# A hybrid attention / S5 / FFN block: more weight and staging buffers in the FFN, a rotated tile order, two products slice by slice

## The chip, the cores and the metric

One Trainium2 chip, one core. The kernel is timed as device microseconds of that core. Its engines are named as in the trace: PE (TensorE matmul) and PEld (its weight loads), DVE (VectorE), ACT (ScalarE), POOL (GpSimd), SP (SyncE, which only issues DMAs here).

## The reference

One encoder block on x of 1024 tokens by 1024 features, all in float32:

```python
h = rms(x, g_pre_mix) * (1 + sc1) + sh1
q_lat, kv_lat, k_rope_raw, u, gates = split(h @ w_in)
branch_a = mla(q_lat, kv_lat, k_rope_raw, ...)      # q = rms(q_lat) @ w_uq, 8 heads: 64 nope + 32 rope
branch_b = s5(u, ...)                                # two scans, then gelu, w_glu
mixed = (sigmoid(gates_a) * branch_a + sigmoid(gates_b) * branch_b) @ w_mix_out
x = x + gt1 * rms(mixed, g_post_mix)
h = rms(x, g_pre_ffn) * (1 + sc2) + sh2
g, up = split(h @ w_ffn_in)                          # 2 x 2816 features, 22 slices of 128
f = (silu(g) * up) @ w_ffn_out
x = x + gt2 * rms(f, g_post_ffn)
```

sc, sh and gt are six vectors of length 1024 computed from a conditioning vector c.

## The kernel before

Everything is held transposed, features on the 128 partitions and tokens along the free axis, in two halves of 512 tokens. A float32 product is three fp32r matmuls (`mm3`, L203 to L205): weight's high part by data's high part, high by the data's low part (L204), and the weight's low part by data's high part (L205). So each weight tile and each operand is split first: the high part by ACT (a copy, `whi`, `fhi`, `mh`), the low part by DVE (a subtraction, `wlo`, `flo`). Each engine runs its instructions in the order in which the code records them, and an instruction that waits holds all that stand behind it.

Weights ahead of the late FFN come through `win`, a stream of the class `WStream` over the list `wl`: `win.get()` hands out the next weight, and on the way splits a further one (L185 on ACT, L67 on DVE) and loads later ones on SP. The list and the order of the `get` calls must agree.

Attention. `uq_nope` and `uq_rope` make the query tiles (four without rotation, two rotated), `kv_norm`, `k_rope` and `y_chain` are generators whose steps are interleaved with them. Then come the k and v products (`uk`, L1106, and `uv`). Behind the heads, the attention-out product takes eight output tiles in two halves, (m, h), and the mix product reads them all.

FFN. The 22 pairs (one slice of gate and one of up) stand in nine groups (`FGROUPS` 4, 2, 2, 2, 2, 2, 2, 2, 4). Group 0 goes plainly through `ffn_in(p, h)`: gate, then up, 24 matmuls each. Its first pair follows directly on `chain`, which makes the eight slices of the normed input (L1575 on ACT, L75 on DVE); between products, `tick()` runs one step of a backlog of such chains and `drain()` runs all that is left. Groups 1 to 8 go through `pair7`: both halves of a pair from seven block products over a split weight and data of half the depth (28 slices of three matmuls), with weight blocks A11, S2, S1, S3, A12, A22 and S4. Sums of weight blocks are POOL's (L1733 to L1744). The class `Blocks` keeps the list of these weight blocks and of the output weights behind each group (`O`, and `L` for the last), splits them (L1717 on ACT, L67 on DVE) some steps ahead, and loads them with DMAs from POOL's queue (L1703) into two raw tiles `wraw`. A raw tile is loaded again once its last block is split.

A pair ends in `ft` tiles (high and low part of the activated product, low half first, then high half; L1619). Behind each group, `out_tiles` multiplies all eight output tiles by the group's two pairs; ACT copies each of the 16 results into one of four staging tiles `fio` (L1661), and a POOL DMA adds it to `fd` in HBM (L1663). The last group's results are read together with `fd`, and finished by `final`: sums of squares (L1875 on ACT, L247 on PE), a norm, and per tile a product (DVE), the addition of x (POOL, L1918) and a store; loads and stores there are issued from ACT's queue (L149). The last group's columns are done in three parts: tokens of half 0, a first 256 of half 1, and the last 256. `drain()` stands between these parts, so that the five remaining steps of half 0's final are recorded ahead of the next part's work.

Of the kernel before, what the change touches and what calls it, by code (L numbers as in the profile page):

```python
# [17 lines left out]
P = 128  # L18
# [73 lines left out]
def _body(tc, a, out):  # L92
# [204 lines left out]
    wl += [(a["wuq"][i], 6 * P) for i in range(3)] + [(a["wuk"], 8 * P), (a["wuv"], 2 * HF)]  # L297
# [774 lines left out]
    def uq_rope():  # L1072

        w = win.get(2)
# [67 lines left out]
    for i in range(4):  # L1142
        if i % 2 == 0:
            w = win.get()
        uq_nope(i, w)
        next(kv_norm, None)
        if i == 2:
            next(krope)
        if i == 2:
            next(ych)  # L1150
    uqr = uq_rope()
    next(uqr)
    for _ in kv_norm:
        pass
    next(ych)
    for _ in uqr:
        next(ych)
# [225 lines left out]
    with ExitStack() as m_es:  # L1383
# [45 lines left out]
        for m in range(KD):  # L1429
            if m >= 4 and m % 2 == 0:  # L1430
                w = [win.get()]
            if m in (2, 4):
                win.split()
            for h in range(2):
                if m < 4:
                    ps = pss[m, h]
                    ao_mm(ps, w[m // 2], m, h, (3,))
                else:
                    ps = ps_b()
                    ao_mm(ps, w[0], m, h, range(4))  # L1440
                ao_out(ps, m, h)
            gm_load(m + 2)
            flush()
# [38 lines left out]
    def prod(ps, w, hi, lo, n, off=0):  # L1482
        for k in range(n):
            mm3(ps, w, hi(k), lo(k), off + k, k == 0, k == n - 1)
            if k % 2:
                tick()

# [134 lines left out]
    def ffn_in(p, h):  # L1622
# [9 lines left out]
        for w, ps in ((wg, pg), (wu, pu)):  # L1632
            prod(ps, w, lambda k: hi[:, k, :], lambda k: lo[:, k, :], KD)
# [7 lines left out]

    def f_tile():
        return half_tile(fp, "fio", 4)
# [38 lines left out]
    class Blocks:  # L1682


        def __init__(self, seq):
            self.seq, self.n, self.got, self.raw, self.hl = seq, 0, 0, [], []
            self.loads = []
            for kind, i, j in seq:
                if kind == "A11":
                    self.loads += [a["wfi"][2 * i], a["wfi"][2 * i + 1]]  # L1690
                elif kind == "O" and j % 2 == 0:
                    o = 2 * starts[i] * P
                    self.loads.append(a["wfo"][j:j + 2, :, o:o + HF].rearrange("m p c -> p m c"))
                elif kind == "L":
                    o = 2 * starts[i] * P
                    self.loads.append(a["wfo"][j, :, o:o + D])

        def load(self, n=1):
            for _ in range(n):
                if self.loads:  # L1700
                    t = wp.tile([P, D], F32, name="wraw", tag="wraw", bufs=2)
                    src = self.loads.pop(0)
                    G.dma_start(t.rearrange("p (m c) -> p m c", m=2) if len(src.shape) == 3 else t, src)  # L1703
                    self.raw.append(t)
# [18 lines left out]
        def advance(self, n):  # L1723

            while self.n < min(n, len(self.seq)):
# [3 lines left out]
                if kind == "A11":  # L1729
                    g, u = self.g, self.u = self.raw.pop(0), self.raw.pop(0)  # L1730
# [16 lines left out]
                elif kind == "S4":  # L1747
                    self.split(self.g[:, hi])
                    self.load(2)
                elif kind == "O":  # L1750
                    self.split(self.raw[0][:, halves[j % 2]])
                    if j % 2:
                        self.raw.pop(0)
                        self.load()
                else:
                    self.split(self.raw.pop(0), self.out() if j == 3 else None)
                    self.load()
# [77 lines left out]

    def pair7(p, prep):
# [21 lines left out]
        A_.activation(gl, gl, AF.Silu)  # L1858
        tt(p1, prod7(tops["T4"]), u3, ALU.add)
        tt(gl, gl, p1, ALU.mult)  # L1860
        ft_put(p, lo, gl)
        tt(u2, prod7(b22), u2, ALU.add)
# [65 lines left out]
    for kind, i, hs in units:  # L1928
# [9 lines left out]
        for m in range(0, KD, 2):  # L1938
            out_tiles(0, win.get(), [(m, h), (m + 1, h)], out_store, m == 0)
            if h and m == 4:  # L1940
                bl.load(2)
# [6 lines left out]
    for g in range(1, last + 1):  # L1948
        big_first = g % 2 == 0
        for n, p in enumerate(range(starts[g], starts[g + 1])):  # L1950
            if (n < 2) == big_first:
                if n % 2 == 0:
                    ft_big(1, p)
            else:
                ft_new(p)
            pair7(p, drain if p == starts[1] else tick)
# [4 lines left out]

    tt(gg2, ada[:, 40:48], g_post2, ALU.mult)
# [7 lines left out]
    for h, c0, n in ((0, 0, HF), (1, 0, QF), (1, QF, QF)):  # L1970
# [25 lines left out]
        drain()  # L1996
# [101 lines left out]
```

## Time and profile before

| | us |
|---|---|
| median of 3 runs | 1700.69 (1699.6 to 1703.08) |
| profiled execution | 1698.5 |
| its span in the trace | 1696.7 |
| PE busy | 1594.6, 94% of the span |
| DVE, ACT, POOL busy | 1084.4, 652.0, 408.9 |
| mean granted clock of TensorE | 0.978 |

The span runs from the first to the last instruction in the trace. A busy PE isn't PE at its peak: matmuls overlap, and each is listed with a modelled end. In a wait row, the time is what the engine stood idle ahead of the instruction; in a timeline row it stands in brackets, with the engine and line that ended it. The granted clock is a fraction of full speed, 1.00 for 2.4 GHz and 0.50 for 1.2 GHz.

### The profile page before, as it was taken

How to read it: one execution, taken by the hardware profiler on the slowest of the kernel's cores; microseconds unless marked ns; L12 is line 12 of the kernel's file. 1: busy time of each engine (PE TensorE's matmuls, PEld its weight loads, DVE VectorE, ACT ScalarE, POOL GpSimd, SP SyncE). 2: the span in 40 equal slices, each digit the busy share in tenths (PEclk: the TensorE clock that was granted, in tenths of full speed). 3: DMA queues.
4: the chain of work that ended last, by engine and by line, in shares of the span. 5: the costliest groups of instructions: out<-in, count | busy, mean ns of one | idle time of the engine just before them, and what ended most of it. 6: DMA issues, size and time to landing. Idle time of an engine off the chain costs nothing.

```text
span 1696.7 us, 20064 instructions
## 1 busy us (share of the span) xinstructions
PE 1594.6 (94%) x7318; PEld 1276.0 (75%) x7318; DVE 1084.4 (64%) x1785; ACT 652.0 (38%) x961; POOL 408.9 (24%) x470
## 2 busy tenths in 40 slices
PE   6989999999899999989999999999999999999994
PEld 6878888888688677757777777777777877777783
DVE  6978998977857778855646676625336335244655
ACT  4142313233621666663334444343333343333330
POOL 0430000012410000001523201243442542533224
PEclk9899999999999999999999999999999999999997
DMA  8143333478896423243432533173763763745154
GB/s 328 63 129 99 109 103 102 141 231 260 291 263 193 100 45 88 45 101 126 160 118 86 181 126 123 64 139 86 123 125 86 137 118 93 137 94 129 50 161 138
DMA packets 111491, 224.32 MB, mean 132 GB/s; under 512 B 22297, under 2 KB 40857, under 8 KB 111393
## 3 DMA queue, kind: packets, MB, share of 16 engines
q1 hardware_dynamic: 55904, 101.75, 20.3%
q0 software_dynamic: 28384, 71.35, 19.0%
q10 hardware_dynamic: 27104, 49.95, 8.4%
q8 instruction: 57, 0.93, 0.2%
q14 instruction: 42, 0.34, 0.1%
HBM read 149.66 MB, written 73.33 MB: 131 GB/s over the span
## 4 chain that ended last, share of the span: by engine, by line
PE 43%; DVE 26%; issue 9%; ACT 8%; DMA 7%; POOL 6%; SPq 1%; ACTq 0%; DVEq 0%; POOLq 0%
PE mm L205 9%; PE mm L204 9%; PE mm L203 9%; DVE t L67 5%; DVE wlo L67 4%; POOL fd L1663 2%; PE sc L1256 2%; PE sc L1257 2%; DVE sq L67 2%; PE sc L1258 2%; PE pv L1282 2%; DMA wraw<-in_wfo 2%; ACT whi L1717 2%; PE pv L1283 2%; PE pv L1281 1%
## 5 line engine op out<-in xcount | busy, mean ns | idle before, releaser
L67 DVE TENSOR_TENSOR wlo<-wraw,whi 128x512 fp32r<-128x512 f32 (+2 forms) x191 | 186.2, 979 | 171.3 <-ACT whi L1717 116.5
L204 PE MATMUL mm<-mh,whi 128*128 128x512 f32 x448 | 177.0, 395 | 4.6 <-DVE mh L75 2.6
L205 PE MATMUL mm<-mh,wlo 128*128 128x512 f32 x448 | 177.0, 395 | 2.8 <-DVE wlo L67 2.7
L203 PE MATMUL mm<-mh,whi 128*128 128x512 f32 x448 | 177.6, 396 | 0.8 <-ACT mh L1408 0.5
L203 PE MATMUL mm<-hhi,whi 128*128 128x512 f32 x384 | 155.3, 404 | 1.3 <-ACT ev L605 1.3
L205 PE MATMUL mm<-hhi,wlo 128*128 128x512 f32 x384 | 152.0, 396 | 0.2 <-DVE wlo L67 0.2
L204 PE MATMUL mm<-hlo,whi 128*128 128x512 f32 x384 | 151.3, 394 | 0.0
L67 DVE TENSOR_TENSOR wlo<-xk,whi 128x512 fp32r<-128x512 f32 x36 | 29.5, 819 | 141.8 <-ACT whi L1717 141.8
L1661 ACT COPY fio<-mm 128x512 f32<-128x512 f32 x128 | 74.0, 585 | 111.7 <-DMA fd<-fio 94.1
L1717 ACT CAST whi<-wraw 128x512 fp32r<-128x512 f32 (+1 forms) x121 | 74.4, 630 | 110.3 <-DMA wraw<-in_wfi 44.3
L1663 POOL DMA_DIRECT2D fd<-fio x112 | 96.4, 1025 | 51.0 <-ACT fio L1661 49.0
L203 PE MATMUL mm<-mr,whi 128*128 128x512 f32 (+1 forms) x236 | 93.9, 398 | 12.2 <-ACT whi L1717 5.9
L204 PEld LDWEIGHTS mm<-mh,whi 128*128 128x128 f32 x448 | 85.0, 190 | 26.7 <-DVE mh L75 5.9
L205 PEld LDWEIGHTS mm<-mh,wlo 128*128 128x128 f32 x448 | 85.0, 190 | 23.1 <-DVE wlo L67 5.4
L203 PEld LDWEIGHTS mm<-mh,whi 128*128 128x128 f32 x448 | 85.1, 190 | 20.4 <-ACT whi L185 1.3
L67 DVE TENSOR_TENSOR plo<-p,phi 128x1024 fp32r<-128x1024 f32 x64 | 78.2, 1223 | 24.5 <-ACT phi L1262 24.0
L204 PE MATMUL mm<-mr,whi 128*128 128x512 f32 (+1 forms) x236 | 90.8, 385 | 1.9 <-DVE mr L67 1.9
L205 PE MATMUL mm<-mr,wlo 128*128 128x512 f32 (+1 forms) x236 | 91.4, 387 | 0.7
L1261 ACT ACTIVATE p<-sc 128x1024 f32<-128x1024 f32 x64 | 65.6, 1025 | 66.8 <-PE sc L1258 56.7
L203 PEld LDWEIGHTS mm<-hhi,whi 128*128 128x128 f32 x384 | 73.1, 190 | 18.0 <-issue 1.8
L205 PEld LDWEIGHTS mm<-hhi,wlo 128*128 128x128 f32 x384 | 72.8, 190 | 16.7 <-DVE wlo L67 0.7
L203 PE MATMUL mm<-fhi,whi 128*128 128x512 f32 (+1 forms) x196 | 77.7, 397 | 8.0 <-ACT fhi L1619 7.8
(584 smaller groups left out, 3844.0 us busy)
## 6 DMA issues: line engine op xcount, KB each, us to landing
fd<-fio POOLq DMA_DIRECT2D x112, 256.0 KB, 5.6
wraw<-in_wfi POOLq DMA_DIRECT2D x36, 512.0 KB, 4.1
wraw<-in_win SPq DMA_DIRECT2D x26, 512.0 KB
wraw<-in_wfo POOLq DMA_DIRECT2D x18, 512.0 KB, 4.2
wada<-in_wada SPq DMA_DIRECT2D x16, 512.0 KB
gdram<-ev ACTq DMA_DIRECT2D x32, 256.0 KB
wraw<-in_wfi SPq DMA_DIRECT2D x16, 512.0 KB
wraw<-in_wmix SPq DMA_DIRECT2D x10, 512.0 KB
```

Of the source, the lines that this page charges most:

```text
L67: return self.eng.tensor_tensor(o, a, b, op=op)
L203: PE.matmul(ps, whi[:, c], rhi, start=first, stop=False)
L204: PE.matmul(ps, whi[:, c], rlo, start=False, stop=False)
L205: PE.matmul(ps, wlo[:, c], rhi, start=False, stop=last)
L1256: PE.matmul(ps[:, c], kh[0:97, kc], qh[0:97, c], start=True, stop=False)
L1257: PE.matmul(ps[:, c], kh[0:96, kc], ql[0:96, c], start=False, stop=False)
L1258: PE.matmul(ps[:, c], kl[0:96, kc], qh[0:96, c], start=False, stop=True)
L1261: A_.activation(p, ps, AF.Exp)
L1282: PE.matmul(ps[0:n, c], vhi[:, kt, q, vc], lo[:, c], start=False, stop=False)
L1661: A_.copy(r, ps)
L1663: G.dma_start(fd[h, m], r, accum_op=ALU.add)
L1717: A_.copy(hi, src)
```

## The change

Five things change. (A) The query weights are taken in another order: two plain tiles, the two rotated ones, then the other two plain ones, with the steps of the generators placed anew. (B) The last four attention-out tiles go by half: (6, 0), (7, 0), (6, 1), (7, 1). (C) In the first pair, `prod2` makes gate and up slice by slice: gate's three matmuls of input slice k, then up's. (D) `Blocks` loads from SP's queue; it has two more raw tiles, and `f_tile` four more staging tiles, in a large tile that is free from the first pair on (`more_room`); the large tile, in which every second group's results stood before, takes only those of the last group's second two pairs (`ft_big`), and the loads from the last group's third pair on use the first two raw tiles alone. In `pair7` the low half's subtraction is recorded behind the next block product. (E) The `drain()` between the two parts of half 1 goes.

```diff
@@ -294,7 +294,7 @@
         units += [("in", p, hs) for p in range(FGROUPS[0])] + [("out", 0, hs)]
 
     wl = [(a["win"][i], KD * P) for i in range(26)]
-    wl += [(a["wuq"][i], 6 * P) for i in range(3)] + [(a["wuk"], 8 * P), (a["wuv"], 2 * HF)]
+    wl += [(a["wuq"][i], 6 * P) for i in (0, 2, 1)] + [(a["wuk"], 8 * P), (a["wuv"], 2 * HF)]
     wl += [(a["wglu"][m], 8 * P) for m in range(KD)]
     wl += [(a["wao"][m], KD * P) for m in range(4)]
     mix0 = len(wl)
@@ -1071,7 +1071,7 @@
...
-        w = win.get(2)
+        w = win.get()
@@ -1139,22 +1139,24 @@
 
     ych, krope = y_chain(), k_rope()
     next(krope)
-    for i in range(4):
-        if i % 2 == 0:
-            w = win.get()
+    w = win.get()
+    for i in range(2):
         uq_nope(i, w)
-        next(kv_norm, None)
-        if i == 2:
-            next(krope)
-        if i == 2:
-            next(ych)
+        next(kv_norm)
     uqr = uq_rope()
     next(uqr)
+    next(kv_norm)
+    next(krope)
+    next(ych)
     for _ in kv_norm:
         pass
+    for _ in uqr:
+        pass
+    w = win.get(2)
+    for i in range(2, 4):
+        uq_nope(i, w)
+        next(ych)
     next(ych)
-    for _ in uqr:
-        next(ych)
     w = win.get()
     uv = uv_tiles(win.get())
     for m in range(4):
@@ -1426,21 +1428,23 @@
             for h in range(2):
                 pss[m, h] = ps_b()
                 ao_mm(pss[m, h], w[m // 2], m, h, range(3))
-        for m in range(KD):
-            if m >= 4 and m % 2 == 0:
+        order = [(m, h) for m in range(KD - 2) for h in range(2)]
+        order += [(m, h) for h in range(2) for m in range(KD - 2, KD)]
+        for m, h in order:
+            if h == 0 and m in (4, 6):
                 w = [win.get()]
-            if m in (2, 4):
+            if h == 0 and m in (2, 4):
                 win.split()
-            for h in range(2):
-                if m < 4:
-                    ps = pss[m, h]
-                    ao_mm(ps, w[m // 2], m, h, (3,))
-                else:
-                    ps = ps_b()
-                    ao_mm(ps, w[0], m, h, range(4))
-                ao_out(ps, m, h)
-            gm_load(m + 2)
-            flush()
+            if m < 4:
+                ps = pss[m, h]
+                ao_mm(ps, w[m // 2], m, h, (3,))
+            else:
+                ps = ps_b()
+                ao_mm(ps, w[0], m, h, range(4))
+            ao_out(ps, m, h)
+            if h and m < KD - 2:
+                gm_load(m + 2)
+                flush()
         ao_low()
     o_es.close()
     v_es.close()
@@ -1484,6 +1488,13 @@
             mm3(ps, w, hi(k), lo(k), off + k, k == 0, k == n - 1)
             if k % 2:
                 tick()
+
+    def prod2(pss, ws, hi, lo):
+
+        for k in range(KD):
+            for ps, w in zip(pss, ws):
+                mm3(ps, w, hi[:, k, :], lo[:, k, :], k, k == 0, k == KD - 1)
+            tick()
 
     def half_tile(pl, nm, bufs=None, n=HF):
         return pl.tile([P, n], F32, name=nm, tag=nm, bufs=bufs or 2)
@@ -1629,7 +1640,9 @@
         c = halves[h]
         pg, pu = ps_b(), ps_b()
         hi, lo = h2t[h]
-        for w, ps in ((wg, pg), (wu, pu)):
+        if p == 0:
+            prod2((pg, pu), (wg, wu), hi, lo)
+        for w, ps in ((wg, pg), (wu, pu)) if p else ():
             prod(ps, w, lambda k: hi[:, k, :], lambda k: lo[:, k, :], KD)
         t = half_tile(c2, "acc0", 1)
         A_.activation(t, pg, AF.Silu)
@@ -1639,7 +1652,13 @@
 
     fio = []
 
+    f_more = []
+
     def f_tile():
+        if f_more:
+            f_more.append(f_more.pop(0))
+            if f_more[-1] is not None:
+                return f_more[-1]
         return half_tile(fp, "fio", 4)
 
     def f_load(h, m, c0=0, n=HF):
@@ -1684,24 +1703,39 @@
 
         def __init__(self, seq):
             self.seq, self.n, self.got, self.raw, self.hl = seq, 0, 0, [], []
-            self.loads = []
+            self.loads, self.live, self.more = [], 0, []
             for kind, i, j in seq:
                 if kind == "A11":
-                    self.loads += [a["wfi"][2 * i], a["wfi"][2 * i + 1]]
+                    self.loads += [(a["wfi"][2 * i + x], i >= starts[last] + 2) for x in range(2)]
                 elif kind == "O" and j % 2 == 0:
                     o = 2 * starts[i] * P
-                    self.loads.append(a["wfo"][j:j + 2, :, o:o + HF].rearrange("m p c -> p m c"))
+                    self.loads.append((a["wfo"][j:j + 2, :, o:o + HF].rearrange("m p c -> p m c"), False))
                 elif kind == "L":
                     o = 2 * starts[i] * P
-                    self.loads.append(a["wfo"][j, :, o:o + D])
-
-        def load(self, n=1):
-            for _ in range(n):
-                if self.loads:
-                    t = wp.tile([P, D], F32, name="wraw", tag="wraw", bufs=2)
-                    src = self.loads.pop(0)
-                    G.dma_start(t.rearrange("p (m c) -> p m c", m=2) if len(src.shape) == 3 else t, src)
-                    self.raw.append(t)
+                    self.loads.append((a["wfo"][j, :, o:o + D], True))
+
+        def load(self):
+
+            while self.loads:
+                src, tail = self.loads[0]
+                if self.live < 2:
+                    t, i = wp.tile([P, D], F32, name="wraw", tag="wraw", bufs=2), None
+                    self.live += 1
+                elif self.more and not tail:
+                    i, t = self.more.pop(0)
+                else:
+                    return
+                self.loads.pop(0)
+                SY.dma_start(t.rearrange("p (m c) -> p m c", m=2) if len(src.shape) == 3 else t, src)
+                self.raw.append((t, i))
+
+        def free(self, *tiles):
+            for t, i in tiles:
+                if i is None:
+                    self.live -= 1
+                else:
+                    self.more.append((i, t))
+            self.load()
 
         def new(self, w):
             if w == D:
@@ -1727,7 +1761,8 @@
                 self.n += 1
                 lo, hi = halves
                 if kind == "A11":
-                    g, u = self.g, self.u = self.raw.pop(0), self.raw.pop(0)
+                    self.gu = self.raw.pop(0), self.raw.pop(0)
+                    g, u = self.g, self.u = [x[0] for x in self.gu]
                     self.split(g[:, lo])
                     self.s1, self.s2 = half_tile(c2, "xk", NXK), half_tile(c2, "xk", NXK)
                     G.tensor_tensor(self.s1, u[:, lo], u[:, hi], op=ALU.add)
@@ -1746,15 +1781,15 @@
                     self.split(self.u[:, hi])
                 elif kind == "S4":
                     self.split(self.g[:, hi])
-                    self.load(2)
+                    self.free(*self.gu)
                 elif kind == "O":
-                    self.split(self.raw[0][:, halves[j % 2]])
+                    self.split(self.raw[0][0][:, halves[j % 2]])
                     if j % 2:
-                        self.raw.pop(0)
-                        self.load()
+                        self.free(self.raw.pop(0))
                 else:
-                    self.split(self.raw.pop(0), self.out() if j == 3 else None)
-                    self.load()
+                    r = self.raw.pop(0)
+                    self.split(r[0], self.out() if j == 3 else None)
+                    self.free(r)
 
         def get(self):
             self.advance(self.got + 1 + self.ahead())
@@ -1832,6 +1867,15 @@
             mm3(ps, w, hi[:, k, :], lo[:, k, :], k, k == 0, k == 3)
             if k % 2:
                 tick()
+
+    def more_room():
+
+        drain()
+        t = row_big(1).rearrange("p k c -> p (k c)")
+        bl.more = [(0, t[:, 0:D]), (1, t[:, D:2 * D])]
+        for i in range(4, 8):
+            f_more.extend([t[:, i * HF:(i + 1) * HF], None])
+        bl.load()
 
     def pair7(p, prep):
 
@@ -1856,10 +1900,13 @@
         tt(u2, ps5, u2, ALU.add)
         tt(gl, prod7(b21), p1, ALU.add)
         A_.activation(gl, gl, AF.Silu)
+        fh, fl = ft[p]
         tt(p1, prod7(tops["T4"]), u3, ALU.add)
         tt(gl, gl, p1, ALU.mult)
-        ft_put(p, lo, gl)
-        tt(u2, prod7(b22), u2, ALU.add)
+        A_.copy(fh[:, lo], gl)
+        ps3 = prod7(b22)
+        tt(fl[:, lo], gl, fh[:, lo].bitcast(F32), ALU.subtract)
+        tt(u2, ps3, u2, ALU.add)
         A_.activation(u2, u2, AF.Silu)
         tt(u2, u2, uh, ALU.mult)
         ft_put(p, hi, u2)
@@ -1938,7 +1985,7 @@
         for m in range(0, KD, 2):
             out_tiles(0, win.get(), [(m, h), (m + 1, h)], out_store, m == 0)
             if h and m == 4:
-                bl.load(2)
+                bl.load()
             if h and m == 4:
                 bl.advance(2)
             if h and m == 6:
@@ -1946,19 +1993,18 @@
     drain()
     backlog.append(tops_3())
     for g in range(1, last + 1):
-        big_first = g % 2 == 0
         for n, p in enumerate(range(starts[g], starts[g + 1])):
-            if (n < 2) == big_first:
-                if n % 2 == 0:
-                    ft_big(1, p)
-            else:
+            if n < 2:
                 ft_new(p)
-            pair7(p, drain if p == starts[1] else tick)
+            elif n == 2:
+                ft_big(1, p)
+            pair7(p, more_room if p == starts[1] else tick)
         if g == last:
             break
         for m in range(0, KD, 2):
             out_tiles(g, bl.get(), [(m + i, h) for h in range(2) for i in range(2)], out_store, m == 0)
 
+    del f_more[:]
     tt(gg2, ada[:, 40:48], g_post2, ALU.mult)
     facc = [big(F32) for _ in range(2)]
     x1s = big(F32)
@@ -1993,7 +2039,9 @@
             for _ in range(TN):
                 tick()
             next(fin)
-        drain()
+            drain()
+        elif not h:
+            drain()
         backlog.append(fin)
     drain()
     ff_es.close()
```

Three places show how instructions move. Names with numbers are tiles. **First pair, PE, before:** the last slice of gate (`mm_7873`, weight `whi_7789`) and the first two of up (`mm_7874`, weight `whi_7859`); `mh_7469` and `mh_7470` are the high and low part of the input.

```order
L203 MATMUL mm_7873<-mh_7469,whi_7789 128x512 [waits Activation_49]
L204 MATMUL mm_7873<-mh_7470,whi_7789 128x512 [waits DVE_49]
L205 MATMUL mm_7873<-mh_7469,wlo_7790 128x512
L203 MATMUL mm_7874<-mh_7469,whi_7859 128x512 [waits Activation_49]
L204 MATMUL mm_7874<-mh_7470,whi_7859 128x512
L205 MATMUL mm_7874<-mh_7469,wlo_7860 128x512 [waits DVE_49]
L203 MATMUL mm_7874<-mh_7469,whi_7859 128x512
```

After the change, PE at the first slice of gate:

```order
L203 MATMUL mm_7873<-mh_7469,whi_7789 128x512 [waits Activation_49]
L204 MATMUL mm_7873<-mh_7470,whi_7789 128x512 [waits DVE_49]
L205 MATMUL mm_7873<-mh_7469,wlo_7790 128x512 [waits DVE_49]
L203 MATMUL mm_7874<-mh_7469,whi_7859 128x512 [waits Activation_49]
L204 MATMUL mm_7874<-mh_7470,whi_7859 128x512
L205 MATMUL mm_7874<-mh_7469,wlo_7860 128x512 [waits DVE_49]
L203 MATMUL mm_7873<-mh_7469,whi_7789 128x512
```

Up's first slice now follows on gate's first, not on its eighth. Where up's weight is split hasn't moved. ACT in the changed kernel, up to that split (before, the same rows stand in the same order, with other line numbers):

```order
L1544 COPY mr1_7179<-mm_7795 128x512 [waits PE_49]
L1514 ACTIVATE sq_7829<-mm_7795 128x512 [waits Pool_49]
L1586 ACTIVATE mh_7469<-ht_7832,ada_77 128x512 [waits DVE_49]
L1586 ACTIVATE mh_7469<-ht_7836,ada_77 128x512 [waits DVE_49]
L1586 ACTIVATE mh_7469<-ht_7840,ada_77 128x512 [waits DVE_49]
L1586 ACTIVATE mh_7469<-ht_7844,ada_77 128x512 [waits DVE_49]
L185 CAST whi_7859<-wraw_7751 128x1024 [waits DMAHW1_49]
```

The split of up's weight (`whi_7859`) stands behind all the steps of the chain that makes the input slices; on DVE, `wlo_7860` likewise stands behind the last of its steps.

**FFN's block stage, POOL, before**, about one group (loads of weights, additions into `fd` and sums of weight blocks):

```order
L1744 TENSOR_TENSOR wraw<-wraw,xk 128x512
L1703 DMA wraw<-in_wfo 128x2x512 x2
L1703 DMA wraw<-in_wfi 128x1024 x2
L1663 DMA fd<-fio 128x512 x4
L1733 TENSOR_TENSOR xk<-wraw 128x512
L1734 TENSOR_TENSOR xk<-xk,wraw 128x512
L1735 TENSOR_TENSOR wraw<-wraw 128x512
L1663 DMA fd<-fio 128x512 x12
L1744 TENSOR_TENSOR wraw<-wraw,xk 128x512
L1703 DMA wraw<-in_wfi 128x1024 x2
```

After, SP (its last rows ahead of the stage and the first of it; `mr_8991` is the large tile):

```order
L1729 DMA wraw<-in_wfi 128x1024 x2
L1684 DMA fd<-fio 128x512 x2
L1729 DMA mr_8991<-in_wfi 128x1024 x2
L1729 DMA wraw<-in_wfo 128x2x512 x2
L1729 DMA mr_8991<-in_wfi 128x1024 x2
L1729 DMA wraw<-in_wfi 128x1024 x2
L1729 DMA mr_8991<-in_wfo 128x2x512 x2
```

The loads left POOL's queue, on which only the additions and the sums stay, and go by turns to the two old and the two new raw tiles.

**The tail, ACT**, a piece of the difference: the squares of the last part's tiles (L1875, now L1922), and the loads and stores of half 1's first part's and half 0's final (L149).

```order
 L149 DMA xk<-x1d 128x512
 L149 DMA out_xt<-mh 128x512
+L1922 ACTIVATE sq<-mh 128x256
 L149 DMA xk<-x1d 128x512
 L149 DMA out_xt<-mh 128x512
 L149 DMA xk<-x1d 128x512
-L149 DMA out_xt<-mh 128x512 x3
-L1875 ACTIVATE sq<-mh 128x256 x3
+L149 DMA out_xt<-mh 128x512
+L1922 ACTIVATE sq<-mh 128x256
+L149 DMA out_xt<-mh 128x512 x2
+L1922 ACTIVATE sq<-mh 128x256 x3
```

The squares, which stood behind all eight stores of half 0, now stand between them.

## Rows read from the trace of the kernel before

**Rows 1.** The page: PE's busy time, its share of the span, its instructions.
```profile
PE 1594.6 (94%) x7318; PEld 1276.0 (75%) x7318; DVE 1084.4 (64%) x1785; ACT 652.0 (38%) x961; POOL 408.9 (24%) x470
```

**Rows 2.** Waits of PE, whole span: engine, line, waited for; total, times, longest us.
```profile
PE mm L247 <- ACT sq L1875: 13.0, 4, 11.0
...
PE mm L203 <- ACT fhi L1619: 7.8, 5, 1.8
PE mm L203 <- ACT whi L1717: 6.6, 12, 0.8
...
PE s L1106 <- DVE qra L67: 5.7, 1, 5.7
PE mm L203 <- ACT mr L1619: 5.5, 3, 1.8
...
PE mm L204 <- POOL mh L1416: 1.9, 2, 1.7
```

**Rows 3.** Timeline, PE inside a pair: start, duration, line, tiles.
```profile
1149.65 0.39 PE L204 MATMUL mm<-mh,whi 128*128 128x512 f32 x1
1149.88 0.39 PE L205 MATMUL mm<-mh,wlo 128*128 128x512 f32 x1
```

**Rows 4.** Timeline of all engines at one hand-over, 1168 to 1183 us.
```profile
1168.18 1.48 POOL L1703 DMA_DIRECT2D wraw<-in_wfo  x2 [1.11 <-issue]
...
1172.34 0.62 ACT L1717 CAST whi<-wraw 128x512 fp32r<-128x512 f32 x1 [4.61 <-DMA wraw<-in_wfo]
...
1172.99 0.69 DVE L67 TENSOR_TENSOR wlo<-wraw,whi 128x512 fp32r<-128x512 f32 x1 [2.62 <-ACT whi L1717]
...
1173.60 0.68 DVE L67 TENSOR_TENSOR acc<-mm,ht 128x512 f32<-128x512 f32 x1
...
1175.36 0.40 PE L203 MATMUL mm<-mr,whi 128*128 128x512 f32 x1
...
1178.95 0.50 PE L204 MATMUL mm<-mr,whi 128*128 128x512 f32 x1 [0.23 <-DVE mr L67]
...
1179.41 0.69 DVE L67 TENSOR_TENSOR sq<-mm,sq 128x512 f32<-128x512 f32 x1
...
1182.19 0.50 PE L203 MATMUL mm<-mr,whi 128*128 128x512 f32 x1 [1.82 <-ACT mr L1619]
...
1182.92 0.50 PE L204 MATMUL mm<-mr,whi 128*128 128x512 f32 x1 [0.22 <-DVE mr L67]
```

**Rows 5.** Windows: stretch, us; busy of PE, PEld, DVE, ACT, POOL; PEclk; DMA, GB/s.
```profile
1250.00:1253.40 3.40, 3.40 (x10) 2.63 (x9) 0.69 (x1) 1.32 (x3) 3.40 (x5) 0.50 0.74 172
...
441.00:447.80 6.80, 3.90 (x9) 3.13 (x10) 6.61 (x9) 4.84 (x7) 2.39 (x1) 0.50 0.55 185
```

**Rows 6.** The page's DMA issues: count, KB each, median us from issue to landing.
```profile
fd<-fio POOLq DMA_DIRECT2D x112, 256.0 KB, 5.6
```

**Rows 7.** Timeline of the first pair, half 0.
```profile
930.00 1.03 ACT L185 CAST whi<-wraw 128x1024 fp32r<-128x1024 f32 x1
...
931.07 2.36 DVE L67 TENSOR_TENSOR wlo<-wraw,whi 128x1024 fp32r<-128x1024 f32 x2
...
932.36 0.48 PE L203 MATMUL mm<-mh,whi 128*128 128x512 f32 x1
```

**Rows 8.** Timeline of the first pair, half 1.
```profile
1003.42 2.36 DVE L67 TENSOR_TENSOR wlo<-wraw,whi 128x1024 fp32r<-128x1024 f32 x2 [0.19 <-ACT whi L185]
...
1003.85 0.39 PE L203 MATMUL mm<-mh,whi 128*128 128x512 f32 x1
...
1004.70 0.50 PE L205 MATMUL mm<-mh,wlo 128*128 128x512 f32 x1 [0.22 <-DVE wlo L67]
```

**Rows 9.** Timeline of ACT and its queue in the tail.
```profile
1662.29 5.08 ACTq L149 DMA_DIRECT2D out_xt<-mh  x3
1667.47 0.78 ACT L1875 ACTIVATE sq<-mh 128x256 f32<-128x256 f32 x2 [11.99 <-POOL mh L1918]
1673.14 0.42 ACT L1875 ACTIVATE sq<-mh 128x256 f32<-128x256 f32 x1 [4.88 <-DVE mh L67]
```

## Prediction

> **What bounds the kernel now.** I read the page first: PE is busy for 94% of the span [rows 1], so a part of the change is worth what it takes from PE's idle time, or adds to it. What one matmul costs is read inside a pair, where nothing waits: each starts 0.23 us behind the last, although it is listed with 0.39 [rows 3]. A wait therefore costs more than its row says: the idle time, plus the 0.16 by which the listed end lies behind the next possible start. Second, the waits of PE [rows 2]: the longest is one of 11.0 us for ACT's squares in the tail (L247, 13.0 in total), then 5.7 at L1106, and three groups of the late FFN: for high parts of activated products (L1619, 7.8 and 5.5) and of weights (L1717, 6.6 in 12 waits). Third, what a wait does to the clock: behind one, stretches stand at a granted clock of 0.50, as at 1250 us, 3.4 us long, and at 441 us, where PE is idle for most of the first half and then runs 9 matmuls in 3.9 us [rows 5]. At that level half of the working time is lost: 1.7 us of 3.4, about 2 after the longer idle.
>
> **D, the block stage, the largest term.** One hand-over from a group's second pair to its output tiles shows the mechanism [rows 4]. POOL issues the output weights at 1168.18, after the last weight block is split. They land 4.2 us later. ACT's copy waits for them 4.61 us, DVE's subtraction stands behind it at 1172.99, and behind that stands work that needs no weight: the low half's addition at 1173.60, and at the end of that row of work the high half's at 1179.41. From its start to PE's first matmul on the high half, at 1182.19, are 2.78 us. PE lost there 1.82 + 0.16 = 1.98 us, then 0.50 at 1182.92 (0.73 behind the last start, not 0.23), and 0.50 at 1178.95 for the low half: 3.0. The seven groups 1 to 7 each hand over once, at 1117, 1182, 1248, 1312, 1377, 1442 and 1509 us: 21 us. After three of these (1117, 1250 and 1509 us) the clock is halved for 3.4 us [rows 5], 1.6 each: 4.8. The twelve waits for weights' high parts [rows 2] stand at the starts of pairs; with 0.16 each, and 0.2 for the low part that follows, they are 6.6 + 4.3 = 10.9.
>
> After the change the same weights are asked for a pair earlier: a raw tile more for each. A pair is 84 matmuls, 84 x 0.23 = 19 us, against 4.2 for a landing. So ACT's and DVE's splits no longer hold what stands behind them. What remains at a hand-over comes from the rows' own durations: the product ahead of the high half's addition ends at about 1175.6 (its last matmul starts 0.23 ahead of the first output matmul, 1175.36). DVE then has one split and the low half's subtraction, now behind that split, ahead of it, 0.61 each: the addition starts some 1.5 us behind the product, at 1177.1, not at 1179.41, and PE can have the high half at 1179.9. It wants it at 1182.19 - 1.98 = 1180.2, so the long wait goes; a wait for a low part, 0.5, may stay, and I keep 0.65 per hand-over, 4.6 in all. In the last group, whose later loads have the two old tiles alone, I leave three of the twelve waits, 2.7. D gives 21 - 4.6 + 4.8 + 10.9 - 2.7 = 29.4; I take 29. Its bounds: 18, if every hand-over keeps half of its 3.0 and no half clock goes (10.5 + 8.2), and 33, if nothing remains but half of what I kept. POOL's 54 issues of 0.74 each (1.48 for two [rows 4]) go to SP, which has nothing else to do there.
>
> In these rows POOL's issue follows the last split at once and nobody waits for POOL itself, so I count the move to SP as nothing and the extra tiles as the whole term. A rule of the Trainium skill speaks against both: by "DMA: Bandwidth & Descriptors", section Issuing engines are not separate DMA queues, DMAs of all queues run on the same 16 engines and interleave, and another issuing engine only saves issue time. By it the move alone would give 0, as I count it, and the earlier loads would stretch the additions that they now meet, which is rival 3; no row here shows the two together.
>
> **C, gate and up slice by slice.** The rows of the order show it: up's first slice now stands second on PE, but its weight is split where it was, behind all steps of the chain. In half 0 its high part is copied from 930.00 to 931.03, and its low part, the first of two, ends at 931.07 + 1.18 = 932.25 [rows 7]. PE, which runs in order, stands there from gate's first slice on. From 932.25 are left 43 of 48 matmuls, 43 x 0.228 = 9.8: 942.1. Before, up began at 932.36 and takes 24 x 0.228 = 5.5: 937.8. (The few sums of squares that stand between are the same in both.) A loss of 4.2 us, and of about 2 more if the clock is halved behind so long an idle, as behind the one at 441 [rows 5]. In half 1 the low part is there at 1003.42 + 1.18 = 1004.60, the end is 1014.4, and before it was 1003.85 + 5.5 + 0.4 for a wait on that low part (0.22 + 0.16): 1009.7 [rows 8]. A loss of 4.7, and again 2. Together 8.9 to 12.9; later waits of this stage, at most 1.5 us, may shrink since PE comes later. I take -11, with bounds of -7 and -14. Nothing hides it: these are PE's only products there.
>
> **E, the tail.** Half 0's final leaves on ACT's queue eight stores and five loads, each pair bound to POOL's additions; the last three stores take 5.08 us, and only then come the next squares, 11.99 late [rows 9]. PE's wait of 11.0 [rows 2] follows. After two squares at 1667.47 comes a third at 1673.14. Now the squares stand between the stores: the first two go while the stores run, and the third behind the last store, at about 1668. So the row that began at 1673.14 begins at 1668.0: 5 us. Bounds: 0, if the additions of half 0 delay DVE and POOL for the new squares by as much, and 8, with the halved clock gone too.
>
> **A and B.** In A, the wait of 5.7 us at L1106 [rows 2] goes, since the rotated tiles' work has two more plain tiles to hide under, and about 2 of half clock with it [rows 5]. But the splits of the k and v weights now stand behind the rotation's 16 steps on DVE, 16 x 0.61 = 9.8 [rows 4], and the first low part takes 1.2 more [rows 7], while PE has 36 matmuls of plain tiles beside it, 8.3: the first `uk` waits 3 at least, with a half clock behind it again, and the later splits and the stores of those two tiles are pushed back by as much. I take 0, with bounds of +2.5 (the waits swap, and the later work is hidden) and -2. In B the addition on POOL that PE waited for, 1.7 of the 1.9 [rows 2], is done a tile earlier; but the next weight's split, right behind it, stays behind all four tiles: -0.5, bounds -1 and +1.
>
> **The sum.** 29 + 5 + 0 - 0.5 - 11 = 22.5 us less. The profiled execution is 1698.5, its span 1696.7 and 1.8 around it; it lies 2.2 below the median of the three runs, 1700.7. 1698.5 - 22.5 = 1676.0 on its scale, 1678.2 on the median's: **1678 us**.
>
> **The rivals.** *1: C costs nothing.* If the chain's steps were done much earlier on ACT and DVE than these rows, or the split stood ahead of them, C would give instead of cost: PE's waits in the chain shrink by up to 5. Then 1678 - 16 = 1662. Against it stand rows 7 and 8 and the order of ACT. *2, slower: the hand-over keeps its wait.* The place is DVE's row of work ahead of the high half's addition. If the new loads still land behind the splits' places, the additions wait as before, and the low half's subtraction, now behind a split, is late by a further 0.7 seven times. D is then 10.9 - 2.7 - 4.9 = 3.3, and -3.1 if the longer waits halve the clock at the other four hand-overs too (4 x 1.6): 1704 to 1710. It decides where D falls 22.5 short of the forecast, below 6.5. For it speaks that one late load is paid on two engines that run in order; against it, 19 us of lead against a landing of 4.2. *3: half of D.* The early loads and the additions (5.6 us each to land [rows 6]) lengthen each other, staging tiles come free late, and ACT's copies hold splits as before: D is 15, the time 1692. *4: A or E fail alone.* 1683 at the most with E at nothing, inside my range.
>
> **How the numbers follow.** Forecast with its own bounds, 1670 to 1685: 0.63. Rival 1: 0.09. Rival 3: 0.14. Rival 4, apart from the forecast: 0.05. Rival 2: 0.09, of which 0.04 within 0.2% of the median (3.4 us, about what a measurement of this kernel can tell) and 0.05 slower. The range from 1661 to 1693 leaves out rival 2 and the far side of rivals 1 and 3. Faster 0.91, same 0.04, slower 0.05.
>
> **What the changed trace would show.** D: no wait for the output weights on ACT between a group's pairs, PE's waits at L1619's successor below 3 us in total, and no half clock behind the hand-overs. C: a wait of PE of several us in the first pair of either half, for ACT's and DVE's split of up, right behind gate's first slice. E: the 11 us wait gone, several small ones in its place. A: the wait at L1106 gone, one for a weight's low part ahead of `uk`. I would be wrong above all if the loads, though early, land late, or if up's split runs ahead of the chain.

## The result, and the profile after

The changed kernel took 1674.08 us in the median of 4 runs (1669.54 to 1676.75) against 1701.88 of before: a ratio of 0.9832, 95% interval 0.9804 to 0.9861. The forecast was 1678. Its profiled execution has a span of 1671.2 us, 25.5 less than before.

PE's waits over the whole span, the answer to [rows 2] (engine, line, waited for; total, times, longest us):

```profile
PE mm L203 <- ACT whi L185: 14.9, 3, 8.7
...
PE mm L247 <- ACT sq L1922: 7.1, 4, 5.3
PE mm L203 <- issue: 5.8, 1, 5.8
...
PE mm L204 <- DVE flo L67: 1.6, 7, 0.2
...
PE mm L203 <- ACT whi L1751: 1.0, 2, 0.8
```

Gone are the waits for the activated products' high parts (7.8 and 5.5) and nearly all of the 6.6 for split weights; the tail's 11.0 is 5.3. New are 14.9 for ACT's splits of weights (L185), 13.5 of it for up's weight in the two halves of the first pair, and 5.8 at the first `uk` product ("issue": the trace names no releaser). The 5.7 at L1106, a line of the `uv` products, are gone.

The same hand-over as in [rows 4], now at 1192 us (timeline):

```profile
1187.96 0.69 DVE L67 TENSOR_TENSOR wlo<-mr,whi 128x512 fp32r<-128x512 f32 x1 [1.21 <-ACT whi L1751]
...
1188.57 0.69 DVE L67 TENSOR_TENSOR flo<-acc,fhi 128x512 fp32r<-128x512 f32 x1
...
1189.17 0.69 DVE L67 TENSOR_TENSOR sq<-mm,sq 128x512 f32<-128x512 f32 x1
...
1191.96 0.51 PE L203 MATMUL mm<-fhi,whi 128*128 128x512 f32 x1
...
1192.68 0.51 PE L204 MATMUL mm<-flo,whi 128*128 128x512 f32 x1 [0.22 <-DVE flo L67]
```

The high half is there in time; only its low part comes 0.5 late (0.72 behind the last start, not 0.23). That repeats at all seven hand-overs and was all that PE lost there. The window that holds all seven (stretch, us, busy of PE, PEld, DVE, ACT, POOL, PEclk, DMA, GB/s) shows no half clock any more:

```profile
1125.00:1500.00 375.00, 373.43 (x1631) 305.38 (x1630) 193.84 (x249) 155.03 (x275) 156.14 (x149) 1.00 0.57 121
```

The first pair, half 0 (timeline, beside [rows 7]):

```profile
932.79 1.03 ACT L185 CAST whi<-wraw 128x1024 fp32r<-128x1024 f32 x1
...
933.87 0.80 PE L203 MATMUL mm<-mh,whi 128*128 128x512 f32 x1 [8.66 <-ACT whi L185]
934.47 0.63 PE L204 MATMUL mm<-mh,whi 128*128 128x512 f32 x1
```

PE stands 8.66 us for ACT's split of up's weight, and its first matmuls afterwards start 0.60 apart, not 0.23. In half 1 the wait is 4.80.

PE runs 7318 matmuls in every kernel of this study, so stages can be measured from the start of one matmul to that of a later one, by their count. The table has such lengths in us; the stages named bound all of the change, and what is missing is not touched by it (it differs by 0.5 us between the two). The tail counts to PE's last matmul; what comes behind takes 9.7 us before and 10.5 after.

| stage (us in the trace of before) | part | before | after | difference |
|---|---|---|---|---|
| query tiles, 413 to 500 | A | 86.9 | 88.7 | +1.8 |
| end of attention-out, 800 to 860 | B | 60.0 | 60.5 | +0.5 |
| first pair: 922 to 945, 998 to 1020, and 1020 to 1060 | C | 85.4 | 95.2 | +9.8 |
| block stage, first pair, 1060 to 1098 | D | 38.5 | 43.6 | +5.2 |
| block stage, the rest, to 1640 | D | 541.6 | 502.7 | -38.9 |
| tail, from 1640 | E | 46.9 | 41.8 | -5.1 |

### The profile page after: what moved, and what is told of

It reads as the page before. It is cut to its first block, busy times and chain, and to the rows that moved or that the text cites. A ratio compares the mean times of both kernels' runs of the same rounds, so it can differ in the third digit from the quotient of the medians.

```text
span 1671.2 us, 20101 instructions
## 1 busy us (share of the span) xinstructions
PE 1586.1 (95%) x7318; PEld 1284.8 (77%) x7318; DVE 1099.8 (66%) x1785; ACT 650.6 (39%) x961; POOL 386.6 (23%) x416
## 4 chain that ended last, share of the span: by engine, by line
PE 58%; DVE 20%; DMA 7%; ACT 6%; issue 4%; POOL 3%; SPq 1%; ACTq 0%; DVEq 0%; POOLq 0%
PE mm L205 14%; PE mm L204 14%; PE mm L203 14%; DVE t L67 4%; DVE wlo L67 2%; PE sc L1258 1%; PE pv L1284 1%; PE sc L1260 1%; ACT whi L185 1%; PE sc L1259 1%; PE pv L1285 1%; PE pv L1283 1%; PE mx L1206 1%; DVE sq L67 1%; PE s L203 1%
## 5 line engine op out<-in xcount | busy, mean ns | idle before, releaser
L67 DVE TENSOR_TENSOR wlo<-wraw,whi 128x1024 fp32r<-128x1024 f32 (+2 forms) x139 | 153.7, 1113 | 106.6 <-ACT whi L185 57.3
L203 PE MATMUL mm<-mh,whi 128*128 128x512 f32 x448 | 180.6, 403 | 15.5 <-ACT whi L185 14.9
L204 PE MATMUL mm<-mh,whi 128*128 128x512 f32 x448 | 178.2, 398 | 1.3 <-POOL mh L1418 1.3
L204 PE MATMUL mm<-flo,whi 128*128 128x512 f32 (+1 forms) x292 | 112.5, 385 | 1.6 <-DVE flo L67 1.6
L203 PE MATMUL mm<-fhi,whi 128*128 128x512 f32 (+1 forms) x292 | 113.7, 389 | 0.0
L205 PE MATMUL mm<-fhi,wlo 128*128 128x512 f32 (+1 forms) x292 | 111.9, 383 | 0.0
L1682 POOL DMA_DIRECT2D fd<-mr x56 | 74.9, 1489 | 118.5 <-ACT mr L1680 117.8
L204 PEld LDWEIGHTS mm<-hlo,whi 128*128 128x128 f32 x384 | 73.4, 191 | 16.0 <-DVE hlo L75 0.6
L67 DVE TENSOR_TENSOR wlo<-mr,whi 128x512 fp32r<-128x512 f32 x52 | 55.2, 1068 | 43.9 <-ACT whi L1751 43.3
L1520 POOL TENSOR_TENSOR acc<-acc,sq 128x512 f32<-128x512 f32 x35 | 49.7, 1427 | 135.5 <-ACT sq L1514 125.0
```

The source lines that it names most:

```text
L67: return self.eng.tensor_tensor(o, a, b, op=op)
L203: PE.matmul(ps, whi[:, c], rhi, start=first, stop=False)
L204: PE.matmul(ps, whi[:, c], rlo, start=False, stop=False)
L205: PE.matmul(ps, wlo[:, c], rhi, start=False, stop=last)
L1520: self.eng.tensor_tensor(self.acc, self.acc, self.q, op=ALU.add)
L1682: G.dma_start(fd[h, m], r, accum_op=ALU.add)
```

## The experiments

Each run was taken beside runs of the kernel before on the same chip; ratios are against those, with 95% intervals. The medians of the kernel before were 1701.9, 1698.1, 1692.5 and 1692.4 in four series of runs; no trace shows why the later ones are lower. The variants do not follow it: each one's time lies within 3.5 us of the change's 1674.08 plus what its stages differ from the change's. So a variant is compared with the change by time and by stage, and a ratio holds for its own series only. The change itself was timed in the first series alone; against 1692.4 its gain would be 18 us, not 28.

**C undone** (gate, then up, for the first pair too):

```diff
-        if p == 0:
-            prod2((pg, pu), (wg, wu), hi, lo)
-        for w, ps in ((wg, pg), (wu, pu)) if p else ():
+        for w, ps in ((wg, pg), (wu, pu)):
```

> Part C undone: gate, then up, in the first pair too; all else as in the changed kernel. Theory: the waits for up's split are what C costs, 12.2 us at the end of the stage by the two traces, of which 2.5 come back soon after; so 1674 - 9.7 = 1664 us, with no wait of PE above 2 us in the first pair. Rival: PE's delay there is swallowed by later waits that shrink in turn; then 1671 to 1674.

Measured: 1663.97 us, 0.9799 (0.9783 to 0.9816). The C stages take 85.4 us, as before the change, and all that follows is as in the changed kernel. C costs 9.8 us in its stages, and nothing downstream swallows it.

**C with up's weight split ahead of the chain's remaining steps:**

```diff
             mix_tile(m, 1, mos[1], sqs[1])
+        win.split()
         drain()
...
         if h and i == 0 and kind == "in":
+            win.split()
             drain()
```

> Part C kept, but up's weight is split ahead of the remaining steps of the chain, not behind them, in both halves. Theory: the order of products is sound and only the place of the split costs; PE then follows the chain slice by slice, 1.37 us of work for each 1.45 us step, and ends the first pair some 5 us ahead of the kernel before in half 0 and 1 us in half 1: 1674 - 9.7 - 6 = 1658 us. Rival: the split ahead of the chain delays every slice by its own 1.1 us and PE is bound by the chain anyway, so that nothing is won over gate then up: 1664 to 1666.

Measured: 1667.85 us, 0.9818 (0.9798 to 0.9837): better than the change (C stages 88.5, not 95.2), worse than gate then up. Both expectations missed. PE's waits of the two halves:

```profile
PE mm L203 <- ACT whi L185: 4.3, 2, 2.9
```

In half 0 the split now starts on ACT at 929.56, right behind the copy and the square of the product in front (928.61 and 929.07). These stand behind two steps of the chain, which wait for DVE (2.28 and 0.72); PE's last matmul of that product started at 926.64. So the split is still late, only by less. A second version follows below.

**D without the two raw tiles** (the line that sets `bl.more` is gone), **without the four staging tiles** (the loop that fills `f_more` is gone), and **without both**:

> Part D without the two further raw weight tiles; the four further staging tiles, the loads on SP and the moved subtraction stay. Theory: late loads held both split engines, so the extra raw tiles are D's gain: some 25 of 34 us are lost, 1699 us, and PE's waits of about 3 us at each hand-over are back. Rival: the staging tiles are D's gain, since ACT's copies waited 94 us for additions into HBM before the change: within 3 us of 1674.

> Part D without the four further staging tiles; the two raw tiles, the loads on SP and the moved subtraction stay. Theory (raw tiles are the gain): ACT's copies wait for additions again, some 90 us in all, but the splits behind them have a pair's lead: 1674 to 1678 us. Rival (staging tiles are the gain): the copies hold the splits behind them on ACT, PE waits at the starts of pairs as before, 1685 to 1700.

> The changed kernel with neither the two raw tiles nor the four staging tiles; loads on SP and the moved subtraction stay. Theory (either kind of tile is enough): ACT's copies wait for additions and the loads are late at once, the hand-over waits of 3 us and the waits at pair starts are back, 20 to 30 us in all: 1695 to 1704. Rival (queue and order make the gain): at most 8 us over 1674.

Measured: 1680.62 us, 0.9891 (0.9870 to 0.9912); 1674.02 us, 0.9857 (0.9832 to 0.9881); 1700.89 us, 1.0052 (1.0033 to 1.0070). The rest of the block stage takes 507.2, 504.4 and 531.3 us, against 502.7 in the change and 541.6 before. Neither expectation of the first run came; of the other two the theory did. One kind of tile alone keeps nearly the whole gain. With neither, 28.6 of the 38.9 us are gone. The other 10.3 stay: PE's wait at a hand-over is 1.2 us, not 1.8, and the clock is halved behind one hand-over, not three. Which of the rest of D does that (the queue, the order of the subtraction, the place of the `ft` tiles) no run separates. (The ratio of this run is above 1 all the same, since it keeps C's loss and the one at the start of the stage, and was taken beside a faster kernel before.)

ACT's groups between 1125 and 1533 us (busy, mean ns, idle before and its releasers) show both causes by themselves. Before, its copies waited 91.2 us for additions into `fd`, and its splits 53.2 for loads:

```profile
L1661 ACT COPY fio<-mm 128x512 f32<-128x512 f32 x105 | 61.0, 586 | 98.9 <-DMA fd<-fio 91.2 <-PE mm L205 7.0
```

Without raw tiles:

```profile
L1751 ACT CAST whi<-wraw 128x512 fp32r<-128x512 f32 x92 | 55.7, 619 | 79.2 <-DMA wraw<-in_wfi 34.4 <-DMA wraw<-in_wfo 23.1 <-POOL wraw L1779 21.7
L1680 ACT COPY fio<-mm 128x512 f32<-128x512 f32 x56 | 32.9, 588 | 33.8 <-PE mm L205 30.0 <-DMA fd<-fio 3.0
```

Without staging tiles:

```profile
L1680 ACT COPY fio<-mm 128x512 f32<-128x512 f32 x112 | 65.1, 587 | 98.7 <-DMA fd<-fio 91.5 <-PE mm L205 5.9
L1751 ACT CAST whi<-mr 128x512 fp32r<-128x512 f32 x47 | 28.4, 620 | 11.8 <-POOL mr L1779 11.8
```

Without both:

```profile
L1680 ACT COPY fio<-mm 128x512 f32<-128x512 f32 x105 | 60.9, 586 | 91.5 <-DMA fd<-fio 83.6 <-PE mm L205 6.9
L1751 ACT CAST whi<-wraw 128x512 fp32r<-128x512 f32 x87 | 52.7, 620 | 64.1 <-DMA wraw<-in_wfi 22.6 <-DMA wraw<-in_wfo 21.4 <-POOL wraw L1779 20.1
```

ACT waits 57.5 us for late loads in the first, 91.5 for additions in the second, and PE hardly notices; only where both stand in one queue is the split late enough for PE to lose 28.6 us. So the hand-over's wait was neither's alone: ACT has slack for one of them.

**D with the loads on POOL's queue again** (`G.dma_start` in `load`):

> The changed kernel with the block stage's weight loads issued from POOL's queue again; raw and staging tiles and the rest as changed. Undoing one kind of tile alone cost the stage only some 1 to 4 us of 34, so the gain has another source or either kind is enough. Theory (either kind is enough, the queue gives nothing): no loss in the groups, and some 4 us won at the stage's start, where SP's first loads stand behind stores that wait for ACT's copies: 1670 us, 0.981 of before. Rival (the queue is the gain, since loads no longer stand among POOL's additions and sums): the hand-over waits of 3 us are back, 1685 to 1700.

**D with the low half's subtraction ahead of the next block product again:**

```diff
         A_.copy(fh[:, lo], gl)
-        ps3 = prod7(b22)
         tt(fl[:, lo], gl, fh[:, lo].bitcast(F32), ALU.subtract)
-        tt(u2, ps3, u2, ALU.add)
+        tt(u2, prod7(b22), u2, ALU.add)
```

> The changed kernel with the low half's subtraction recorded ahead of the next block product again. Theory: the subtraction has the same neighbours within 0.6 us either way, and the result stays within 3 us of 1674. Rival: the order is what took the hand-over wait away, since a subtraction that waits for ACT no longer holds the weight's split: 1685 or more, with waits for high parts at each hand-over.

Measured: 1666.83 us, 0.9837 (0.9818 to 0.9856), and 1668.53 us, 0.9850 (0.9834 to 0.9866): by ratio both like the change, by time 7.3 and 5.6 us below it. By time, neither expectation of the second run came. The stages show what each wins. With POOL's queue the rest of the block stage stays at 503.2, and its first pair takes 36.6, not 43.6. SP's queue in the changed kernel shows why:

```profile
1072.23 3.09 SPq L1684 DMA_DIRECT2D fd<-fio  x2
1075.42 0.87 SPq L1729 DMA_DIRECT2D wraw<-in_wfi  x2
```

The stage's first two loads stand on SP behind group 0's stores, which wait for ACT's copies, and go at 1075.42; on POOL they went at 1068.00 and 1071.44:

```profile
1068.00 0.58 POOL L1729 DMA_DIRECT2D wraw<-in_wfi  x1
```

With the subtraction first, the rest of the block stage takes 497.8, 4.9 us less than the change: between 1100 and 1610 us PE has no wait in its table at all. The moved subtraction was the 0.50 at each hand-over: it stood behind a split that waited 1.21 for ACT, so the next steps on DVE all came later.

**A version from these:** A, B and C undone, and the first two loads on POOL's queue; then the same with the subtraction first.

```diff
-                SY.dma_start(...)
+                q = SY if self.n else G
+                q.dma_start(...)
```

> D and E alone (A, B and C undone), and the first two weight loads of the block stage on POOL's queue, as before, all others on SP. Theory: C's 8 to 10 us, A's 1.8 and B's 0.5 by the traces, and 4 to 5 us at the stage's start, where the first loads no longer stand behind six stores on SP: 1674 - 15 = 1659 us, 0.974 of before. Rival: the wait at the stage's start is DVE's and ACT's chain there and stays whichever queue loads: 1663 to 1665.

> D and E without A, B and C, the first two loads of the block stage on POOL's queue, and the low half's subtraction ahead of the next block product as before. Theory: the moved subtraction costs 0.50 us at each of seven hand-overs and some more in the last group; without it the block stage runs with no wait of PE at a hand-over: 5 us below the same kernel with the moved subtraction, 0.973 of before. Rival: what is won at the hand-overs is taken back by a weight that is split 0.6 us later: 0.976 as there.

Measured: 1654.47 us, 0.9759 (0.9738 to 0.9781), and 1650.68 us, 0.9751 (0.9726 to 0.9777). Both beat both kernels. The block stage's first pair takes 36.8 in either; the rest 502.3 and 497.9. The 4.4 us of the stage are clear in the traces, and too few for the times to tell the two apart.

**That version with C, and up's weight split ahead of ACT's copy of the product in front:**

```diff
+        if h and m == KEEP0 - 1:
+            win.split()
         A_.copy(mo[:, m, :], ps)
...
+            if not h and m == KD - 2:
+                win.split()
```

> As e18_best_low, with gate and up of the first pair slice by slice (part C), and up's weight split still earlier: ahead of ACT's copy of the product in front, for which the split waited in e2_C_early_split. Theory: PE no longer waits for up's weight, follows the chain, and ends the first pair 3 to 6 us earlier than gate then up in half 0, 1 us in half 1: 0.970 to 0.971 of before. Rival: PE's many short waits for the chain keep the clock at one half for some us, and the chain itself is 1.2 us later: no gain, 0.973 to 0.975.

Measured: 1651.27 us, 0.9760 (0.9736 to 0.9784): no gain. The first pair's half 0 takes 22.6 us, not 23.0, and half 1 the same 22.2. The split now stands right behind a chain step that waits for DVE, and PE still waits 2.0 us once for it; from 929.6 to 933.0 us the granted clock is at its half level, 1.2 GHz (busy and clock as above):

```profile
929.60:933.00 3.40, 3.40 (x10) 2.64 (x9) 3.33 (x5) 1.42 (x2) 0.67 (x1) 0.50 0.40 154
```

In this trace, what the order of products could win from the chain's waits goes into this wait and the half clock behind it.

**A, B and E undone:**

> The changed kernel with A, B and E undone, which lie in stages of their own, so that the trace tells them apart. Theory: the query stage is some 2 us shorter, the attention-out stage 0.5 us, and the tail 5 us longer, with PE's wait of 11 us back: 1677 us, 0.985 of before. Rival for E: the tail's wait is taken over by the last stores, and the end comes no later: 1671 to 1672.

Measured: 1675.35 us, 0.9904 (0.9879 to 0.9930). The tail takes 47.3 us, not 41.8, with a wait of 11.3 back; the query stage 87.2, not 88.7; attention-out 60.7, not 60.5. E is worth 5.4 by this pair of traces. By time the run is 1.3 us above the change, where these three stages give 4.1. The ratio is much higher than the change's own, 0.9832, since the kernel before took only 1692.4 us beside it. Against the version with the subtraction first, which was run beside the same runs of the kernel before, the time is 24.7 us longer, and the stages give 9.7 (C) + 6.6 (the block stage's first pair) + 4.4 (subtraction) + 5.9 (tail) = 26.6.

## Why the prediction was right, step by step

**C** was the loss that it was said to be: it cost 9.8 us where 11 were forecast, with the mechanism in the rows (waits of 8.66 and 4.80, the half clock behind both). 11.0 was lost in the pair itself, 1.2 came back in the stretch to 1060.

**E** was 5.1 where 5 was forecast; undone, it costs 5.4. The mechanism is the one named: two squares now run between the stores, at 1638.84 and 1641.77, and PE's wait for squares is 5.3, not 11.0. Its size is less sure than the two pairs make it look: over all traces the tail takes 41.1 to 44.6 us with E, 42.5 in the mean, and 46.9 and 47.3 without.

**D** was 33.7 net where 29 was forecast, but its parts were not as written, and that it came so near is in part luck: the groups gave 9.9 us more than the sum, and the stage's start took 5.2 that the sum had at nothing. The groups' 38.9 lie above the bound of 33. The sum counted the waits at hand-overs, at pair starts and the half clock, and left out the shorter delays around them: before, 50 matmuls of the groups start 0.26 to 0.35 us behind the last, not 0.23, which makes 5.5 us, and in the changed kernel 8 do. The 5.2 were given back where the prediction says that SP "has nothing else to do there": SP has group 0's stores, and the first loads stand behind them. The prediction takes "the extra tiles as the whole term" and explains them by loads that come early. That was half of it, since ACT's copies had waited for additions all along. The runs show that late loads alone cost 4.5 us, waiting copies alone 1.7, and both together 28.6 (531.3 against 502.7); 10.3 of the 38.9 are not the tiles at all. The 0.65 us kept per hand-over was about right, 0.50 at the low part and 0.11 at the matmul behind it, and was of the change's own making.

**A** cost 1.8 where 0 was taken, inside its bounds: the wait at L1106 went, and one of 5.8 with a half clock took its place, longer than the 3 that was the least. It stands where the prediction has it, at the first `uk` product (438.80). ACT splits that product's weight at 437.67, behind the rotation's last high part at 437.13; so it is the high part of the weight that PE waits for, where the prediction names the low part. Over all traces of the study the query stage takes 88.1 us in the mean with A (8 traces, 87.2 to 90.1) and 86.6 without (5 traces, 85.8 to 87.2): 1.5. **B** cost 0.5 in the first pair of traces, as forecast and by the waits that were named: the one for POOL fell from 1.9 to 1.3, and one of 1.4 for the next weight's split is new. In the others it is within the spread (60.1 to 62.8 with it, 59.7 to 60.7 without); its size stays open.

The rivals: that C costs nothing, that the hand-over keeps its wait, and that half of D is lost to longer additions didn't come. The additions did lengthen, from 5.6 us [rows 6] to 7.8 from the new staging tiles and 8.4 from the old (DMA issues: count, KB, us to landing; the changed kernel, then the run without the new staging tiles):

```profile
fd<-fio POOLq DMA_DIRECT2D x56, 256.0 KB, 8.4
...
fd<-fio POOLq DMA_DIRECT2D x112, 256.0 KB, 5.5
```

Rival 3 gives the early loads as the cause, and they are not: with them and four staging tiles an addition takes 5.5 us, and without the raw tiles, but with eight staging tiles, 8.1 and 8.9. So it goes with the eight staging tiles, which let more additions be under way at once; that their number under way is the reason is not shown. Twice as many tiles also cover it: PE's waits in the groups didn't grow. By the Trainium skill's "DMA: Bandwidth & Descriptors", section Issuing engines are not separate DMA queues, DMAs of all queues interleave on the same 16 engines, and another issuing engine only saves issue time. The trace agrees on the second: the run on POOL's queue takes 503.2 us in the groups, the change 502.7. That interleaving with the early loads stretches an addition, as the prediction drew from the first, these runs don't show (5.5 us against 5.6).

## What to carry to other kernels

When two causes fill one in-order queue, an experiment that removes either shows nearly the whole gain, and only the one that restores both shows what they cost: test them together before one gets the credit. Before products are interleaved, look where each operand is made ready: a weight whose split is recorded behind a chain makes PE wait for all of the chain. And a DMA moved to another queue takes its place behind what is there, at the first issue too.

## What was not expected of the hardware

The same short waits are followed by the half clock in one run and not in another. In the first pair with gate ahead of up, PE waits for low parts of the chain, 0.48, 1.39 and 0.48 us in a row. The run with C undone and the version from the experiments with the subtraction first have these three waits alike to 0.01 us. Behind them the granted clock falls to its half level, 1.2 GHz, for 3.4 us in the first; in the second it stays at 2.4 GHz:

```profile
933.70:937.10 3.40, 3.25 (x9) 2.04 (x8) 3.16 (x6) 2.60 (x3) 0.00 (x0) 0.50 0.52 163
...
929.40:932.80 3.40, 2.69 (x11) 1.34 (x9) 3.16 (x6) 2.62 (x3) 0.00 (x0) 1.00 0.51 173
```

What decides between the two no run shows. The seven hand-overs of the changed kernel, with one wait of 0.22 us each, leave it at 2.4 GHz over 375 us.
